# Attention exponentials kept in PSUM, normalised at once and turned by DMA; GpSimd splits the queries and most weights

## The chip, the cores and the metric

The kernel runs on one core of one Trainium2 chip. The time is device microseconds for one execution; the median of three runs of the kernel before is 1127.67 us (1126.69 to 1128.68). In the text PE is TensorE, DVE is VectorE, ACT is ScalarE, POOL is GpSimd and SP is the queue (SyncE) from which most transfers are issued. Each of these works through its own list of instructions in a fixed order and waits where an operand or a buffer is not ready.

## The reference

Two layers of a transformer trunk for 512 latent tokens (an 8 x 64 grid) and 256 context tokens, width 1024. In each layer the tokens are normalised, modulated and multiplied by one wide matrix; its columns feed two parallel attentions and their gates:

```python
px = hx @ w_in
a_k, a_v, b_k, b_v, a_q, b_q, a_z, b_z, g_a, g_b = _split(px, SPLIT_SIZES)
# A: 8 heads of 64, QK-norm; a latent query sees a window of 8 x 16 grid keys
#    with a learned bias, and all 256 context keys
p = jax.nn.softmax(concatenate([s_win, s_ctx]), axis=-1);  a_att = p @ values
# B: 8 query heads, 2 key/value heads, rotary; a latent query sees all 768 keys
s = einsum(q, k) * HEAD_DIM ** -0.5;  p = softmax(s);  b_att = p @ v
o_a = (a_att * silu(a_z)) @ w_o_a;   o_b = (b_att * silu(b_z)) @ w_o_b
merged = sigmoid(g_a) * o_a + sigmoid(g_b) * o_b
x = x + gate * (merged @ w_out)
```

In layer 0 the context tokens are updated too, so their queries (256) attend to the context keys in both branches. In layer 1 only the latent tokens go on. The result has to hold float32 accuracy, so every operand of a product is split into a high and a low half, and a product is two or three matmuls.

## The kernel before, in words

**Stages.** Each layer runs through the projections of keys, values and queries of branch A, the neighbourhood attention (called NA here; in the profile 149.5 to 305.4 us in layer 0 and 771.5 to 881.7 us in layer 1), the projections of branch B, the grouped attention (called GQ; 382.6 to 549.2 us and 938.2 to 1061.3 us), and the merge with the output projection.

**Fill.** PE does not wait for a softmax: `pipeline` (L997) goes over the eight heads, issues the scores of head h, the values of head h-1, and between them a share of `fill`, a list of pieces of projections that nobody needs yet (the gates z, the sigmoid gates g, the output projection of A). A piece is 24 matmuls of 512 or 256 columns (12 for the output projections) into one bank of PSUM (`psf`, `psx`), then an evacuation by ACT and DVE. Its weights come by DMA from the SP queue (`load_w2`, L410): `raw` (three buffers), a rounding copy `whi` on ACT (L418), and the remainder `wlo` = raw - whi (L420), on DVE and POOL in turn (`mix_lo`, L426).

**Order.** The program is written as above, and a planner that simulates the engines then orders the instructions of each engine. Therefore the order of a changed program can differ everywhere.

**NA, one head** (`na_scores`, L938). Four tiles of 128 queries. For each: two matmuls of 512 columns make 256 window scores and 256 context scores in a bank of the pool `pss` (three banks); DVE adds the bias, negates and takes the extreme in one pass from PSUM to an SBUF tile `p` (L958), which frees the bank; ACT does the exponential in place with the row sum (L961); `softmax_tail` scales by half the reciprocal sum, on DVE (L765) or POOL (L768). `na_values` (L968) turns the tiles: three groups of four 128 x 128 blocks go through PE against the identity (L777, L779) into `pst`, and ACT and DVE split each group into a high and a low half (`transpose_split`, L771). Twelve matmuls follow. In layer 0 `ctx_scores` and `ctx_values` do the same for 256 context queries (one group of four blocks). `head_out` (L789) adds the two halves of the result and multiplies it into the gate.

**GQ, one head** (`gq_scores`, L1122). Four tiles of 128 queries by 768 keys, each in a two-bank buffer of `pss` (two buffers). DVE reads it once for the maximum (L1131, it writes a copy that the next line overwrites), ACT writes the exponentials to SBUF (L1132). `turned` (L799) copies them to half precision on ACT (L802), takes the remainder on DVE or POOL in turn (L803), and a DMA transpose from the SP queue (L804) turns both halves. The sums are applied late: `divide` (L806) takes the reciprocals through PE, four blocks for each head and two for the context queries (L811), and multiplies them into the gate on DVE (L812). `shrink` (L815) scales the values of B so that they fit half precision.

**Staging.** `stage_k` and `stage_q` (L840, L849) split the keys and queries of a head: two copies of K (one DVE, one ACT), a remainder on POOL; a copy of Q on ACT and a remainder on DVE (L855).

**PSUM** has eight banks: one `psf`, two `pst` (both for the whole kernel), and five that are dealt out anew for each stage.

## Time and profile before

| | us |
|---|---|
| median of the runs | 1127.67 |
| the profiled execution | 1127.56 |
| its span, first to last instruction | 1125.6 |
| busy: PE / DVE / ACT / POOL | 1093.3 / 774.7 / 579.0 / 490.6 |
| NA, layer 0: length, PE busy | 155.9, 155.9 |
| GQ, layer 0 | 166.6, 151.8 |
| NA, layer 1 | 110.2, 108.7 |
| GQ, layer 1 | 123.1, 118.0 |

A line of the profile names the source line, the engine, the operation, output and inputs with their shapes, the count, then the busy time and the mean of one in ns, and behind the second bar how long the engine had waited just before, and for whom. Matmuls are pipelined: a row of 400 ns is the time through the array, and the next matmul starts before it ends; what one costs is the distance from start to start. A table by windows gives, for each stretch, its length, the busy time of PE, of its weight loads, of DVE, ACT and POOL with the number of instructions, the granted clock, and the share of the DMA engines.

### The profile page before, as it was taken

To read this page: it belongs to the slowest core of one execution; us is meant where nothing else is said; L and a number is where in the kernel's file an instruction comes from. 1 tells how busy PE (TensorE), PEld (TensorE's weight loads), DVE (VectorE), ACT (ScalarE), POOL (GpSimd) and SP (SyncE) were. 2 spreads that over 40 slices of the span, in tenths; PEclk is the share of its full clock that TensorE was granted. 3 is DMA by queue.
4 is the path that set the end of the run, shared out by engine and by line. 5 is a ranking of instruction groups with operands and counts; after the bars stand their busy time and mean duration, and the time that the engine had idled before them with its cause. 6 is when DMAs were issued, how large, how long until landed. Compare 5 with 4: busy or idle time off the path is not lost.

```text
span 1125.6 us, 16862 instructions
## 1 busy us (share of the span) xinstructions
PE 1093.3 (97%) x5826; PEld 905.3 (80%) x5826; DVE 774.7 (69%) x1492; ACT 579.0 (51%) x1154; POOL 490.6 (44%) x405
## 2 busy tenths in 40 slices
PE   8999999999999999979999999999999999999998
PEld 5688888888998877757788888888888987776677
DVE  4666788897466477776577785458878765677473
ACT  6453266665433576755330284326666446776431
POOL 1054254654247144454521545235554563563531
PEclk9999999999999999989999999999999999999999
DMA  9454322242351488869633532553333236989742
GB/s 373 143 172 140 114 63 66 73 136 89 93 168 38 123 201 185 185 172 269 173 108 125 183 129 72 142 174 92 100 107 116 59 105 172 188 224 239 197 145 80
DMA packets 192222, 161.29 MB, mean 143 GB/s; under 512 B 116364, under 2 KB 158088, under 8 KB 190472
## 3 DMA queue, kind: packets, MB, share of 16 engines
q1 hardware_dynamic: 184800, 145.82, 46.8%
q0 software_dynamic: 2368, 7.87, 2.1%
q10 hardware_dynamic: 4968, 6.53, 1.7%
q8 instruction: 46, 0.75, 0.3%
q14 instruction: 40, 0.33, 0.1%
HBM read 115.58 MB, written 17.32 MB: 118 GB/s over the span
## 4 chain that ended last, share of the span: by engine, by line
PE 38%; issue 4%; DVE 3%; DMA 3%; POOL 2%; ACT 1%; SPq 1%; POOLq 0%; ACTq 0%
PE psx L435 6%; PE psx L433 6%; PE psx L434 6%; PE psf L433 4%; PE psf L434 4%; PE psf L435 4%; PE pss L955 1%; PE pss L861 1%; POOL wlo L406 1%; PE pss L862 1%; PE pst L779 1%; PE pst L1148 1%; DMA raw<-in_w_o_a_dram 1%; PE pst L1149 1%; DMA raw<-in_w_in_dram 1%
## 5 line engine op out<-in xcount | busy, mean ns | idle before, releaser
L420 POOL TENSOR_TENSOR wlo<-raw,whi 128x512 fp32r<-128x512 f32 x70 | 97.9, 1405 | 106.1 <-ACT whi L418 70.4
L433 PE MATMUL psf<-hx,whi 128*128 128x512 f32 (+1 forms) x360 | 138.0, 383 | 3.2 <-ACT zt L614 2.4
L435 PE MATMUL psf<-hx,wlo 128*128 128x512 f32 (+1 forms) x360 | 135.8, 377 | 0.0
L434 PE MATMUL psf<-hx,whi 128*128 128x512 f32 (+1 forms) x360 | 135.1, 375 | 0.0
L433 PE MATMUL psx<-whi,hx 128*128 128x512 f32 (+1 forms) x328 | 120.8, 372 | 0.0
L434 PE MATMUL psx<-wlo,hx 128*128 128x512 f32 (+1 forms) x328 | 119.6, 366 | 0.0
L435 PE MATMUL psx<-whi,hx 128*128 128x512 f32 (+1 forms) x328 | 119.5, 365 | 0.0
L418 ACT CAST whi<-raw 128x512 fp32r<-128x512 f32 x136 | 82.3, 620 | 64.0 <-DMA raw<-in_w_in_dram 35.3
L406 POOL TENSOR_TENSOR wlo<-raw,whi 128x512 fp32r<-128x512 f32 x40 | 61.2, 1535 | 122.1 <-ACT whi L403 80.1
L803 POOL TENSOR_TENSOR h<-p,h 128x768 f16<-128x768 f32 (+1 forms) x40 | 65.7, 1644 | 96.4 <-ACT h L802 72.0
L403 ACT CAST whi<-raw 128x512 fp32r<-128x512 f32 x88 | 54.1, 623 | 99.2 <-PE psx L435 34.2
L420 DVE TENSOR_TENSOR wlo<-raw,whi 128x512 fp32r<-128x512 f32 x66 | 73.6, 1115 | 30.6 <-ACT whi L418 29.0
L504 POOL TENSOR_TENSOR ss<-ss,ehalf 128x8 f32<-128x8 f32 (+2 forms) x40 | 62.5, 1566 | 72.9 <-DVE ss L501 72.8
L433 PEld LDWEIGHTS psf<-hx,whi 128*128 128x128 f32 x360 | 67.9, 188 | 15.4 <-ACT zt L614 3.7
L435 PEld LDWEIGHTS psf<-hx,wlo 128*128 128x128 f32 x360 | 67.8, 188 | 11.6
L1131 DVE CUSTOM_DVE_ANT_0 p<-pss,vb 128x768 f32<-128x768 f32 x64 | 60.3, 953 | 23.6 <-PE pss L862 21.1
L434 PEld LDWEIGHTS psf<-hx,whi 128*128 128x128 f32 x360 | 67.9, 189 | 10.3
L1132 ACT ACTIVATE p<-pss,mx 128x768 f32<-128x768 f32 x64 | 57.6, 900 | 34.7 <-DVE mx L1131 33.7
L435 PEld LDWEIGHTS psx<-whi,hx 128*128 128x128 f32 x328 | 61.9, 189 | 10.0
L434 PEld LDWEIGHTS psx<-wlo,hx 128*128 128x128 f32 x328 | 62.0, 189 | 9.2
L433 PEld LDWEIGHTS psx<-whi,hx 128*128 128x128 f32 x328 | 61.8, 189 | 8.9
L435 PE MATMUL psx<-hx,wlo 128*128 128x256 f32 (+1 forms) x208 | 68.0, 327 | 0.0
(362 smaller groups left out, 3095.8 us busy)
## 6 DMA issues: line engine op xcount, KB each, us to landing
raw<-in_w_in_dram SPq DMA_DIRECT2D x168, 256.0 KB, 2.9
rawb<-in_w_ada_dram SPq DMA_DIRECT2D x48, 256.0 KB, 2.8
raw<-in_w_out_dram SPq DMA_DIRECT2D x32, 256.0 KB, 2.9
tg<-gs SPq DMA_DIRECT2D x4, 1536.0 KB, 6.8
rawx<-in_w_ada_dram SPq DMA_DIRECT2D x4, 1024.0 KB, 9.8
rawy<-in_w_ada_dram SPq DMA_DIRECT2D x4, 1024.0 KB, 9.5
gs<-zt ACTq DMA_DIRECT2D x16, 256.0 KB, 2.0
raw<-in_w_o_a_dram SPq DMA_DIRECT2D x16, 256.0 KB, 3.4
```

Source lines behind the costliest of these rows:

```text
L403: S.copy(hi[:, :n], raw[:, :n])
L406: e.tensor_tensor(lo[:, :n], raw[:, :n], F(hi[:, :n]), ALU.subtract)
L418: S.copy(hi, raw)
L420: lo_eng(i).tensor_tensor(lo, raw, F(hi), ALU.subtract)
L433: T.matmul(ps, lhs[0], rhs[0], start=first, stop=False)
L434: T.matmul(ps, lhs[0], rhs[1], start=False, stop=False)
L435: T.matmul(ps, lhs[1], rhs[0], start=False, stop=last)
L504: G.tensor_tensor(ss, ss, ehalf[:, :n], ALU.pow)
L779: T.transpose(pt[:, c0:c0 + 128], src, ident)
L803: eng.tensor_tensor(h[:, 1], p[:, :n], h[:, 0], ALU.subtract)
L1131: V.tensor_tensor_reduce(p, pss, lift, -1.0, 3e38, ALU.add, ALU.min, mx[:, 0:1])
L1132: S.activation(p, pss, AF.Exp, bias=mx[:, 0:1], accum_out=r[:, i:i + 1])
```

## The change

- **NA.** The biased scores and the exponentials stay in the `pss` bank. DVE takes the reciprocal of the sum and multiplies it by 2^14; ACT writes the normalised high half in half precision to SBUF, DVE the remainder, both from PSUM; a DMA transpose from SP turns them (five for each head: the edge tile in two pieces of 64 rows; one more for the context queries in layer 0). The PE transposes and `softmax_tail` are gone. The values of A are kept in half precision, scaled like those of B (`size`, `shrink`, `halves`). Sixteen value matmuls instead of twelve, on the same columns.
- **GQ.** Two tiles of queries share a buffer of three banks (two buffers); one DVE reduction takes both maxima; the exponentials stay there, and are normalised and split as in NA, all remainders on DVE. `divide` is gone. `pst` has one bank in this stage.
- **Values.** `head_out` applies the common scale of the values. The context values of a head are issued after the fill instead of before.
- **Engines.** The remainder of Q goes to POOL; the second copy of K goes from DVE to ACT; for the gates and the output projection of A every `wlo` is made on POOL.

```diff
-    def evac_va(dsts):            # ACT copy, DVE remainder, both float32
+    def size(v, junk, mx):
+        S.activation(junk, v, AF.Abs)
+        V.tensor_reduce(mx, junk, AX, ALU.max)
+    def shrink(mx, s, row):
+        pt = psw(512, "t")
+        T.transpose(pt[0:1, 0:128], mx, ident)
+        V.tensor_reduce(row, pt[0:1, 0:128], AX, ALU.max)
+        T.matmul(pt[:, 128:129], row.to_broadcast([1, 128]), ident[0:1, 0:1], start=True, stop=True)
+        V.tensor_scalar(s[:, 1:2], pt[:, 128:129], 1.0e-30, 1.0 / V_UP, ALU.max, ALU.mult)
+        V.reciprocal(s[:, 0:1], s[:, 1:2])
+        V.tensor_scalar(s[:, 1:2], s[:, 1:2], 0.5 / P_UP, None, ALU.mult)
+    def halves(v, d, s):
+        S.activation(d[:, :, 0, :], v, AF.Copy, scale=s)
+        V.scalar_tensor_tensor(d[:, :, 1, :], v, s, d[:, :, 0, :], ALU.mult, ALU.subtract)
...
-            return fill_chunks(col0, None, gs[c], False, mix_lo)
+            return fill_chunks(col0, None, gs[c], False, pool_lo)
-                    st["w"] = load_w2(src, 256 * i, 4, pool_lo if br == "b" and i == 0 else mix_lo)
+                    st["w"] = load_w2(src, 256 * i, 4, pool_lo if br == "a" or i == 0 else mix_lo)
-        fill = fill_chunks(C_AZ, lambda: za, None, True, mix_lo) + fill_chunks(C_BZ, None, zs, True, mix_lo)
+        fill = fill_chunks(C_AZ, lambda: za, None, True, pool_lo) + fill_chunks(C_BZ, None, zs, True, pool_lo)
...
+    def evac_va(t, ps):
+        S.copy(vf[:, t, :], ps)
+        size(ps, vab[:, 512 * t:512 * t + 512], vmx[:, t:t + 1])
+    def split_va():               # after the first query projection
+        V.tensor_reduce(vmx[:, 6:7], vmx[:, 0:6], AX, ALU.max)
+        shrink(vmx[:, 6:7], vsa, vsa[0:1, 2:3])
+        for t in range(0, 6, 2):
+            halves(vf[:, t:t + 2, :].rearrange("p t (h d) -> p (t h) d", d=64),
+                   va[:, t:t + 2].rearrange("p t h q d -> p (t h) q d"), vsa[:, 0:1])
...
-                S.copy(a, po[o:o + 64, :n])
-                V.tensor_tensor(a, po[m:m + 64, :n], a, ALU.add)
+                S.activation(a, po[o:o + 64, :n], AF.Copy, scale=back[o:o + 64])
+                V.scalar_tensor_tensor(a, po[m:m + 64, :n], back[m:m + 64], a, ALU.mult, ALU.add)
-            def turned(p, n, out, eng):
+            def turned(p, r, cuts, out):
                 h = att["p"].tile([128, 2, n], F16, tag="h", name=nm("h"), bufs=att["nh"])
-                S.copy(h[:, 0], p[:, :n])
-                eng.tensor_tensor(h[:, 1], p[:, :n], h[:, 0], ALU.subtract)
-                nc.sync.dma_start_transpose(out, h.rearrange("p a n -> p (a n)"))
+                for i, (c0, c1) in enumerate(cuts):
+                    V.reciprocal(r[:, i:i + 1], r[:, i:i + 1])
+                    V.tensor_scalar(r[:, i:i + 1], r[:, i:i + 1], P_UP, None, ALU.mult)
+                    S.activation(h[:, 0, c0:c1], p[:, c0:c1], AF.Copy, scale=r[:, i:i + 1])
+                    V.scalar_tensor_tensor(h[:, 1, c0:c1], p[:, c0:c1], r[:, i:i + 1], h[:, 0, c0:c1],
+                                           ALU.mult, ALU.subtract)
+                for o, n0, n1 in out:
+                    nc.sync.dma_start_transpose(o, h[n0:n1].rearrange("p a n -> p (a n)"))
-            def divide(ps, r, e, dst, back):
-            def softmax_tail(p, n, r, pieces, eng=None):
-            def transpose_split(blocks, n0=0, n1=512):
...
-                V.tensor_copy(rows(kh, e), k)
+                S.copy(rows(kh, e), k)
-                V.tensor_tensor(rows(qs, 1 - e), q, F(rows(qs, e)), ALU.subtract)
+                eng.tensor_tensor(rows(qs, 1 - e), q, F(rows(qs, e)), ALU.subtract)   # eng = G
...
             def na_scores(h, q, kh, kl):
-                    p = p_tile()
-                    V.tensor_tensor_reduce(p[:, :512], pss, bedg if i == 0 else bint, -1.0, 3e38,
-                                           ALU.add, ALU.min, mx[:, 0:1])
-                    S.activation(p[:, :512], p[:, :512], AF.Exp, bias=mx[:, 0:1], scale=-1.0, accum_out=r[:, 0:1])
-                    softmax_tail(p, 512, r[:, 0:1], [(0, 512)], G if i in NA_POOL else None)
+                    V.tensor_tensor_reduce(p, p, bedg if i == 0 else bint, -1.0, 3e38,
+                                           ALU.add, ALU.min, mx[:, 0:1])        # p is the PSUM bank
+                    S.activation(p, p, AF.Exp, bias=mx[:, 0:1], scale=-1.0, accum_out=r[:, 0:1])
+                    at = [(0, 64, 0), (448, 512, 64)] if i == 0 else [(128 * i - 64, 128 * i + 64, 0)]
+                    turned(p, r, [(0, 512)], [(ht[:, :, a:b], n, n + b - a) for a, b, n in at])
...
-            open_ps(s=(2, 1024), v=(1, 512))
+            open_ps(t=1, s=(2, 1536))
             def gq_scores(q, kh, kl):
-                for i in range(4):
-                    V.tensor_tensor_reduce(p, pss, lift, -1.0, 3e38, ALU.add, ALU.min, mx[:, 0:1])
-                    S.activation(p, pss, AF.Exp, bias=mx[:, 0:1], accum_out=r[:, i:i + 1])
-                    turned(p, 768, ht[:, i], G if i in SPLIT_POOL else V)
+                for j in range(2):                       # two query tiles in one buffer
+                    V.tensor_reduce(mx, ps.rearrange("p (i n) -> p i n", i=2), AX, ALU.max, negate=True)
+                    for i in range(2):
+                        S.activation(p, p, AF.Exp, bias=mx[:, i:i + 1], accum_out=r[:, i:i + 1])
+                    for i in range(2):
+                        turned(ps[:, 768 * i:768 * i + 768], r[:, i:i + 1], [(0, 768)], [(ht[:, 2 * j + i], 0, 128)])
...
                     st = scores_of(h)
-                    if prev is not None:
-                        values_of(h - 1, prev)
+                    rest = values_of(h - 1, prev) if prev is not None else None
                     run(fill, len(fill) - (n - n * min(h + 1, spread) // spread))
+                    if rest is not None:
+                        rest()                           # the context values
```

More of the change, by code (lines that the diff above doesn't have):

```diff
@@ L759, in layer, with head_out @@
         if True:
[L760 to L789 removed]
+            def head_out(po, e, dst, back, eng=None):
                 n = dst.shape[-1]
@@ L909, in p_tile, with ctx_values @@
-            def p_tile():
-                return att["p"].tile([128, att["w"]], F32, tag="p", name=nm("p"), bufs=att["np"])
+                turned(p, r, [(0, 256), (256, 512)], [(ct.rearrange("p a i k n -> p (a i k) n"), 0, 128)])
+                return ct
+            def ctx_values(ct, vsl, dst, e, back, kind):
+                po = psw(256, kind)
+                for k in range(2):
+                    for a in range(2):
+                        T.matmul(po.rearrange("p (i n) -> p i n", i=2), vsl(4 + k), ct[:, a, :, k, :],
+                                 start=k + a == 0, stop=k + a == 2)
+                head_out(po, e, dst, back)
@@ L993, in na_values @@
+                for t, part in enumerate((((0, 192, 0),), ((64, 192, 1), (192, 320, 0)),
+                                          ((192, 320, 1), (320, 448, 0)), ((320, 512, 1),))):
+                    for n0, n1, k in part:
+                        for a in range(2):
+                            T.matmul(po[:, n0:n1], vsl(t), ht[:, 4 * a + k, n0:n1], start=False,
+                                     stop=t == 3 and a == 1)
                 zv = za.rearrange("p (f n) -> p f n", f=4)
-                head_out(po, e, zv[64 * e:64 * e + 64, h // 2, 0:512], V if h == 7 else G)
+                head_out(po, e, zv[64 * e:64 * e + 64, h // 2, 0:512], vsa[:, 1:2], V if h == 7 else G)
```

238 lines of the change are left out of this document (74 added, 164 removed).

## The prediction

> **What bounds the kernel now.** I read the busy shares first, then a table by windows over the four attentions, then PE's waits.
>
> ```profile
> PE 1093.3 (97%) x5826; PEld 905.3 (80%) x5826; DVE 774.7 (69%) x1492; ACT 579.0 (51%) x1154; POOL 490.6 (44%) x405
> ```
> ```profile
> 149.50:305.40 155.90, 155.90 (x977) 139.22 (x976) 123.15 (x272) 94.01 (x212) 75.67 (x74) 1.00 0.28 87
> 382.60:549.20 166.60, 151.77 (x845) 121.08 (x843) 114.91 (x205) 104.80 (x203) 75.17 (x54) 0.97 0.80 188
> 771.50:881.70 110.20, 108.72 (x595) 93.04 (x594) 93.92 (x186) 72.46 (x151) 57.31 (x57) 1.00 0.33 102
> 938.20:1061.30 123.10, 117.96 (x555) 88.42 (x554) 80.98 (x128) 83.59 (x149) 65.87 (x44) 1.00 0.91 208
> ```
> ```profile
> PE psv L811 <- DVE ho L796: 5.8, 1, 5.8
> PE psf L433 <- ACT zt L614: 4.0, 5, 1.6
> ```
>
> PE is busy throughout both NA stages, and idle for 14.8 us in GQ of layer 0 and 5.1 us in GQ of layer 1. So a matmul removed shortens the kernel by its own distance from start to start, as long as DVE and ACT keep up. In NA, DVE is the second (79% and 85%). The largest single wait, 5.8 us, has this cause:
>
> ```profile
> 492.20 8.26 DVE L420 TENSOR_TENSOR wlo<-raw,whi 128x512 fp32r<-128x512 f32 x1
> ...
> 501.67 0.42 DVE L796 TENSOR_TENSOR ho<-psv,ho 64x256 f32<-64x256 f32 x1
> ```
> ```profile
> 491.54 7.15 POOL L657 TENSOR_TENSOR gal<-za,gah 128x768 fp32r<-128x768 f32 x4
> ```
> ```profile
> 495.00:510.00 15.00, 9.20 (x34) 6.44 (x33) 11.46 (x11) 3.66 (x7) 8.41 (x7) 0.72 0.67 174
> ```
>
> One DVE subtraction with two SBUF operands stood for 8.26 us while POOL worked through four of its own; behind it stood the `head_out` that frees the bank PE wanted. The granted clock then fell to 0.72.
>
> **PE work removed.** The instructions on the identity, by stage, and the distances from start to start:
>
> ```profile
> 149.50:305.40 155.90, 25.40 (x160) 19.34 (x160) 0.00 (x0) 1.00 0.28 87
> 382.60:549.20 166.60, 8.32 (x49) 5.69 (x49) 0.00 (x0) 0.97 0.80 188
> 771.50:881.70 110.20, 18.19 (x128) 14.91 (x128) 0.00 (x0) 1.00 0.33 102
> 938.20:1061.30 123.10, 4.79 (x32) 3.70 (x32) 0.00 (x0) 1.00 0.91 208
> ```
> ```profile
> 247.97 0.28 PE L991 MATMUL psv<-pth,va 128*128 128x256 f32 x1
> 248.09 0.26 PE L992 MATMUL psv<-pth,va 128*128 128x192 f32 x1
> 248.18 0.60 PE L779 MATMUL pst<-ident,p 128*128 128x128 f32 x4
> 248.54 0.48 PE L955 MATMUL pss<-kh,qs 128*128 128x512 f32 x1
> ...
> 250.68 0.39 PE L434 MATMUL psf<-hx,whi 128*128 128x512 f32 x1
> 250.91 0.40 PE L435 MATMUL psf<-hx,wlo 128*128 128x512 f32 x1
> ```
>
> Four transposes take 0.36 us, 0.09 each; 512 columns take 0.23, 256 take 0.12, 192 take 0.09. Transposes: 160 in NA of layer 0 (14.4 us), 128 in layer 1 (11.5), and 48 (one of the 49 belongs to the gates) and 32 from `divide` (4.3 and 2.9). Added: a head's value matmuls were four of 512, four of 192 and four of 256 columns (1.76 us); now four of 512, four of 192 and eight of 128. A 128-column half-precision matmul is in no row; its bounds are 0.06 (a quarter of 512 columns) and 0.09 (192 columns, or a transpose of 128). I take 0.09, the nearest row: 2.0 us, +0.24 a head, +1.9 us a stage. Net on PE: -12.5, -9.6, -4.3, -2.9.
>
> **What a softmax tile now costs DVE and ACT.** The nearest rows, from the groups of NA in layer 1 by shape:
>
> ```profile
> L958 DVE CUSTOM_DVE_ANT_0 p<-pss,bint 128x512 f32<-128x512 f32 x24 | 15.9, 684 | 0.1
> ...
> L762 DVE RECIPROCAL r<-r 128x1 f32<-128x1 f32 x32 | 4.6, 156 | 2.1 <-ACT p L961 1.7
> L796 DVE TENSOR_TENSOR ho<-psv,ho 64x512 f32<-64x512 f32 x6 | 4.1, 682 | 0.6 <-ACT ho L795 0.4
> ...
> L958 DVE DVE_READ_ACCUMULATOR2_ANT mx<- 128x1 f32 x32 | 2.6, 81 | 0.0
> ```
> ```profile
> L961 ACT ACTIVATE p<-p,mx 128x512 f32<-128x512 f32 x32 | 23.0, 720 | 13.7 <-DVE mx L958 13.6
> L418 ACT CAST whi<-raw 128x512 fp32r<-128x512 f32 x20 | 12.1, 616 | 3.3 <-PE psf L434 3.3
> L785 ACT CAST pth<-pst 128x512 fp32r<-128x512 f32 x14 | 7.6, 587 | 0.1
> ...
> L844 ACT CAST kh<-ka 64x768 fp32r<-64x768 f32 x6 | 5.0, 835 | 3.9 <-PE pss L955 3.9
> ```
>
> An NA tile costs DVE 0.68 + 0.08 + 0.16 for the reciprocal, the same for the multiplication by 2^14, and 0.68 for the remainder (from PSUM, as `head_out`): 1.76 us, and 1.93 with a quarter of `head_out`. It costs ACT 0.72 + 0.59 and a quarter of a head's two K copies (0.84 each), Q copy (512 columns, like `whi`, 0.62) and `head_out` copy (like `pth`, 0.59): 2.03 us. Results in PSUM instead of SBUF are in no row: an engine may write there faster or slower, and I take the same durations, because the rows that read from PSUM (684 and 587 ns) stand within 5% of those that read from SBUF with the same columns (616; 682 has one operand in each). The chain of one tile, from scores to remainder, is the sum of its steps, 3.1 us. DVE loses its `wlo`, its Q remainder, one K copy and the scaling on SBUF, and with them the operations that POOL can hold up. POOL gains the Q remainders and 28 `wlo` a layer and loses the scaling and the remainders of GQ; at 49% and 52% in NA it has room for them, and the fill is loaded two pieces ahead.
>
> **NA, layer 0: -11.5.** A head now takes PE some 18 us. ACT had 94.0 us in the stage, 11.8 a head, and gains a K copy and a fourth tile copy: 13.2; DVE, at 15.4 a head, loses more than it gains. So PE stays the bound. In the order of the changed program, fill stands between scores and values up to the last head: after the last tile of head 7 come 8 us of other PE work. The chain from that tile is 0.46 us of matmuls, 3.1 us of steps and 4.2 us of DMA (below), which leaves nothing for the hand-overs between engines. I count 1 us for them: -12.5 + 1.
>
> **NA, layer 1: +6.** Here the new order matters. Between the first scores and the last values 241 fill matmuls are left of 288; 47 now stand before the first scores, where they cost the same. Heads 0 to 3 take most of the rest (67 us of PE work). After the values of head 3 come 13 tiles and the values of four heads with only one piece of 24 x 256 columns among them (2.9 us): 16.7 us of PE work. The tiles go at 2.0 us each on DVE and ACT, 26 us, and then a transpose (4 us) and the last values (2 us): 32 us. So PE idles about 15 us where it had 1.5; with 1 to 2 us for ACT in the first part, -9.6 + 16 = +6. ACT has 62 us there by the rows above (19 exponentials, 18 tile copies, 27 `whi`, 12 evacuations at 0.62, the K and Q copies of five heads, four `head_out`) against 67 of PE. The bounds are -9.6 (ACT and DVE catch up earlier) and +18 (ACT holds up the first part as well).
>
> **GQ.** A pair of tiles now costs one reduction over 1536 columns, two exponentials, two copies and two remainders:
>
> ```profile
> L1131 DVE CUSTOM_DVE_ANT_0 p<-pss,vb 128x768 f32<-128x768 f32 x64 | 60.3, 953 | 23.6 <-PE pss L862 21.1 <-POOL h L803 1.8
> ...
> L874 DVE TENSOR_REDUCE mx<-pss 128x2 f32<-128x512 f32 x16 | 11.0, 686 | 3.4 <-PE pss L862 3.3
> ```
> ```profile
> L804 SPq DMA_TRANSPOSE ht<-h x64: 1274/1678/7132, 388.6 to 1051.1; - x64
> ```
> ```profile
> ht<-h SPq DMA_TRANSPOSE x64, 4.2
> ```
>
> The reduction is between 0.95 (768 columns) and 2.06 us (three times 512); from 512 to 768 each column costs 1.04 ns, which gives 1.75. DVE then has 1.75 + 2 x (0.95 + 0.32) = 4.3 us a pair against 2 x 1.03 and one remainder of 0.95 before, 2.5 more a head; a head's `wlo`, Q remainder and `divide`, which it loses, are some 0.7 to 1 us each: even. ACT's work is the same. The steps of a pair (reduction, two exponentials of 1.5 x 0.72, reciprocals, two copies of 1.5 x 0.59, one remainder) make 7 us, so a buffer is held 8; the order puts 7 to 13 us of PE work between two uses of one, and it is free in time. In layer 0: -4.3, less the 5.8 us wait (its DVE subtraction is gone) and 2.6 us of low clock (0.28 of 9.2), plus 2.7 for `head_out` (1.3 us and its place in two queues), which now stands between two uses of the single `pst` bank, eight times, with 2.8 to 5.5 us of fill: -10 (bounds -15 and +3). In layer 1 the last pair has 8.8 us of PE work behind it, and its chain, 7 us and 4.2 to land, takes some 12 with the hand-overs: -2.9 + 3 = 0 (bounds -4 and +5).
>
> **Elsewhere: +1.** `size`, `split_va` and ACT's `Abs` stand in projections where PE is the bound; PE's two small steps in `shrink` have 4 us of matmuls between them. 0 to +3.
>
> **Sum.** -11.5 + 6 - 10 + 0 + 1 = -14.5. The profiled execution took 1127.56 us, 0.1 below the median of 1127.67: 1113.
>
> **Rivals.**
> 1. *Everything hidden.* If ACT and DVE run ahead of PE in NA of layer 1, its 15 us of idle do not appear: 1098. For it: PE idled 1.5 us there before, and a bunched order need not be a late one if the engines are quicker than I take them. Against: 13 tiles at 2.0 us have only 16.7 us of PE work beside them.
> 2. *The PSUM chain sets the pace* (slower). Before, a score bank was free after one DVE pass of 0.68 us; now it is held through five steps on two engines in turn, 3.1 us and their hand-overs. It decides if the waits in ACT's in-order list stretch a tile from 2.0 to 2.5 us in layer 1 and a head from 13 past 18 us in layer 0. Then layer 0 gains nothing (+12 on the sum) and layer 1 loses 18 (12 more): 1113 + 24 = 1137. For it: in NA of layer 1 ACT has 92% of PE's time in the first part.
> 3. *The SP queue.* 88 more transposes at 1.68 us are 148 us on the queue that also issues every weight load, and each waits there for its remainder; in NA of layer 1 five take 8.4 of a head's 13 us. If the weights of each of 16 heads come 1.2 us late for PE, that is 19 us: 1132. Against: in GQ four a head have stood among loads for 15 us a head.
>    The Trainium skill (VectorE: DVE Perf Modes, "Rules for kernel authors") says to turn 128 x 128 on TensorE when the result may go to PSUM, and by DMA otherwise; its table of the three paths gives 390 ns and 1309 ns. By its figures the two halves of 288 blocks would cost 754 us of DMA against 112 on PE; the trace has twelve blocks landing in 4.2 us, so only the direction of the rule is left, in this rival.
> 4. *No gain on PE.* If a 128-column half-precision matmul cost 0.20 us, a head's values would take 2.9 us and eat most of the transposes: 0.9 x 16 = 14 us on the sum, 1127. Against: a transpose with 128 columns takes 0.09.
>
> **How the numbers follow.** Chances: forecast 0.48, rival 1 0.22, rival 2 0.17, rival 3 0.08, rival 4 0.05. Faster is the forecast and rival 1: 0.70; same (within 0.2%, 2.3 us, about what a measurement of this kernel can tell from no change) rival 4: 0.05; slower 0.25. The forecast's own range is 1103 to 1122; the range over the cases reaches from just under rival 1 to just under rival 2: 1096 to 1136.
>
> **What would show it.** In the windows: NA of layer 0 near 144 us with PE full; in layer 1 a stretch of some 30 us before the first projection of B with PE half idle and waiting for DMA `ht` or for DVE and ACT on `pss`; no DVE instruction of several us in GQ; no wait above 2 us on `pst`. Wrong would be: PE waits on `raw` or `wlo` in NA (rival 3), DVE or ACT rows on PSUM well above those used here (rival 2), or layer 1 without the idle stretch (rival 1).

## The result, and the profile after

The changed kernel takes 1139.07 us (median of four runs, 1137.48 to 1141.67) against 1127.69 for the kernel before beside it: a ratio of 1.0103, 95% interval 1.0082 to 1.0124. It is slower by 1%, where 1113 was forecast. The profiled execution is the slowest of the four (1141.67); its span is 1139.6 us, 14.0 more than before, where the medians differ by 11.4.

Line 1 of the page of the changed kernel, and its table by windows from the first scores to the last values of NA and GQ in layer 0, then in layer 1 (length; busy time of PE, its weight loads, DVE, ACT, POOL; granted clock; DMA share; GB/s):

```profile
PE 1067.9 (94%) x5528; PEld 857.5 (75%) x5528; DVE 698.8 (61%) x1498; ACT 626.1 (55%) x1208; POOL 485.2 (43%) x389
```
```profile
154.60:305.60 151.00, 140.92 (x863) 118.35 (x862) 100.23 (x280) 104.54 (x226) 68.85 (x57) 0.99 0.76 167
...
378.80:542.90 164.10, 148.68 (x809) 115.26 (x807) 111.66 (x234) 110.97 (x212) 58.13 (x45) 0.98 0.86 194
...
778.50:886.90 108.40, 90.93 (x452) 68.92 (x451) 65.14 (x176) 78.03 (x152) 49.08 (x36) 0.91 0.80 176
...
948.40:1075.20 126.80, 112.11 (x504) 80.22 (x503) 81.24 (x131) 86.80 (x147) 51.68 (x41) 0.99 0.87 201
```

PE's work did fall, by 25.4 us (1093.3 to 1067.9). Its idle time rose by 39.4 (span less busy: 32.3 to 71.7). The lengths of the stages mislead, because the planner moved fill from one stage to the next; length less PE busy does not. Against the forecast's terms (the profiled executions; the forecast's -5.7 for GQ of layer 0 holds 2.6 us of low clock, which the measured columns have under busy):

| term of the sum | forecast, us | measured, us | off by |
|---|---|---|---|
| PE busy, all stages | -29.3 | -25.4 | 3.9 |
| PE idle, NA of layer 0 | +1 | +10.1 | 9.1 |
| PE idle, GQ of layer 0 | -5.7 | +0.6 | 6.3 |
| PE idle, NA of layer 1 | +15.6 | +16.0 | 0.4 |
| PE idle, GQ of layer 1 | +2.9 | +9.6 | 6.7 |
| PE idle, elsewhere | +1 | +3.1 | 2.1 |
| sum | -14.5 | +14.0 | 28.5 |

PE's waits in the changed kernel, longest in total first (total, times, longest):

```profile
PE pst L931 <- DMA ht<-h: 12.1, 3, 6.7
PE psf L429 <- ACT zt L617: 10.1, 10, 2.4
PE pss L912 <- DVE h L798: 5.6, 5, 3.1
PE psf L429 <- DVE tg L695: 4.4, 5, 2.0
PE pst L1094 <- DVE ho L787: 4.0, 1, 4.0
```

**NA, layer 0.** Three times PE stands at `psf` for more than 1 us (2.25, 1.10 and 1.28 of the 5.3 us there), and each time ACT's list shows the same picture. From the timeline of the changed kernel:

```profile
194.55 0.66 ACT L917 ACTIVATE pss<-pss,mx 128x512 f32<-128x512 f32 x1 [4.63 <-DVE mx L914]
...
195.23 0.82 ACT L818 CAST kh<-ka 64x768 fp32r<-64x768 f32 x1
...
196.08 0.83 ACT L819 CAST kh<-ka 64x768 fp32r<-64x768 f32 x1
...
196.93 0.84 ACT L829 CAST qs<-qa 64x768 fp32r<-64x768 f32 x1
...
199.60 0.58 ACT L617 ACTIVATE zt<-psf 128x512 f32<-128x512 f32 x1
...
200.35 0.69 DVE L619 SCALAR_TENSOR_TENSOR zt<-zt,psf 128x512 f32<-128x512 f32 x1
```
```profile
201.09 0.50 PE L429 MATMUL psf<-hx,whi 128*128 128x512 f32 x1 [2.25 <-DVE zt L619]
```

The next head's two K copies and its Q copy run 2.5 us in a row on ACT, and the evacuation that gives PE its bank back comes after them (in this case after an exponential, a `head_out` copy and a context exponential as well). Just before, ACT had been idle for 4.63 us: its load was not the limit. Before the change, the first K copy was on DVE.

**NA, layer 1.** The tail, in windows and in its last tile:

```profile
844.30:886.90 42.60, 25.13 (x122) 15.82 (x122) 25.80 (x71) 26.39 (x52) 11.21 (x8) 0.76 0.74 140
850.00:880.00 30.00, 17.36 (x72) 9.86 (x72) 21.54 (x64) 21.04 (x43) 9.18 (x7) 0.77 0.78 142
```
```profile
866.53 15.34 SPq L801 DMA_TRANSPOSE ht<-h  x8
...
877.10 0.70 DVE L914 CUSTOM_DVE_ANT_0 pss<-pss,bint 128x512 f32<-128x512 f32 x1 [2.21 <-PE pss L912]
...
879.86 0.75 DVE L798 SCALAR_TENSOR_TENSOR h<-pss,r,h 128x512 f16<-128x512 f32 x1 [0.81 <-ACT h L797]
...
883.78 1.86 PE L931 MATMUL pst<-ht,va 128*128 128x512 f16 x4 [6.72 <-DMA ht<-h]
```

As forecast in kind: 30 us in which PE is busy for 17.4 and DVE and ACT for 21 each, and the last values behind the transposes. The first row is the whole stretch behind the values of head 3, 42.6 us long.

**GQ, layer 0.** The 8.26 us DVE instruction is gone, and a wait of the same form stands elsewhere: now ACT's list is behind a late weight, and the `head_out` that frees `pst` behind that. The weight was issued at 478.75 and landed 12.4 us later, where the median of its line is 3.1; ahead of it on SP stood two loads of the gates (`tg`, 1.5 MB each, landed by 488.9), not transposes.

```profile
477.32 1.33 SPq L663 DMA_DIRECT2D tg<-gs  x2
478.75 0.38 SPq L411 DMA_DIRECT2D raw<-in_w_o_a_dram  x1
...
491.16 0.62 ACT L414 CAST whi<-raw 128x512 fp32r<-128x512 f32 x1 [3.15 <-DMA raw<-in_w_o_a_dram]
491.69 0.87 ACT L1079 ACTIVATE pss<-pss,mx 128x768 f32<-128x768 f32 x1
...
492.70 0.47 ACT L786 ACTIVATE ho<-pst,vb 64x256 f32<-64x256 f32 x1
...
493.75 0.51 PE L1094 MATMUL pst<-ht,vb 128*128 128x512 f16 x1 [3.96 <-DVE ho L787]
```

**GQ, layer 1.** One pair of tiles at the end of the stage, from its reduction to its second remainder:

```profile
1057.34 1.75 DVE L1075 TENSOR_REDUCE mx<-pss 128x2 f32<-128x1536 f32 x1
...
1064.39 0.90 ACT L797 ACTIVATE h<-pss,r 128x768 f16<-128x768 f32 x1
...
1065.32 1.02 DVE L798 SCALAR_TENSOR_TENSOR h<-pss,r,h 128x768 f16<-128x768 f32 x1
1066.38 0.90 ACT L797 ACTIVATE h<-pss,r 128x768 f16<-128x768 f32 x1 [1.09 <-DVE h L798]
...
1067.31 1.02 DVE L798 SCALAR_TENSOR_TENSOR h<-pss,r,h 128x768 f16<-128x768 f32 x1 [0.97 <-ACT h L797]
...
1068.47 0.47 PE L429 MATMUL psx<-gbh,whi 128*128 128x512 f32 x1 [2.58 <-DVE h L798]
```

The pair takes 11.0 us (1057.34 to 1068.33), where the forecast had 7 to the first remainder and 8 to the second. It is no exception: over the 16 pairs of this stage the median is 10.5 us (8.5 to 14.1), over those of layer 0 10.1. Two things are new. ACT waits with the copies while its list stands at a `head_out`, and the second tile's copy waits until the first tile's remainder has ended, although it reads other columns: the two tiles share the middle bank. The Trainium skill (PSUM — Partial Sum Buffer, "PSUM bank collisions raise a hardware error") says that two engines may not touch one bank in the same quadrant of 32 partitions at once, reads included, and that the compiler back end's scheduler adds a dependency between two such instructions. The wait of 1.09 us agrees with it.

### The profile page after: what moved, and what is told of

Its sections match the earlier page's. It is cut to its first block, busy times and chain, and to the rows that moved or that the text cites. A ratio compares the mean times of both kernels' runs of the same rounds, so it can differ in the third digit from the quotient of the medians.

```text
span 1139.6 us, 16576 instructions
## 1 busy us (share of the span) xinstructions
PE 1067.9 (94%) x5528; PEld 857.5 (75%) x5528; DVE 698.8 (61%) x1498; ACT 626.1 (55%) x1208; POOL 485.2 (43%) x389
## 5 line engine op out<-in xcount | busy, mean ns | idle before, releaser
L416 POOL TENSOR_TENSOR wlo<-raw,whi 128x512 fp32r<-128x512 f32 x126 | 166.1, 1333 | 131.4 <-ACT whi L414 77.5
L798 DVE SCALAR_TENSOR_TENSOR h<-pss,r,h 128x768 f16<-128x768 f32 (+2 forms) x160 | 127.0, 801 | 36.8 <-ACT h L797 34.8
L429 PE MATMUL psf<-hx,whi 128*128 128x512 f32 (+1 forms) x360 | 137.6, 382 | 12.4 <-ACT zt L617 9.6
L797 ACT ACTIVATE h<-pss,r 128x768 f16<-128x768 f32 (+2 forms) x160 | 114.2, 729 | 26.1 <-DVE h L798 15.7
L402 POOL TENSOR_TENSOR wlo<-raw,whi 128x512 fp32r<-128x512 f32 x40 | 59.5, 1489 | 130.2 <-ACT whi L399 86.0
L1075 DVE TENSOR_REDUCE mx<-pss 128x2 f32<-128x1536 f32 x32 | 55.9, 1754 | 42.4 <-PE pss L837 42.3
L431 PEld LDWEIGHTS psf<-hx,wlo 128*128 128x128 f32 x360 | 68.2, 189 | 12.4
L429 PE MATMUL psx<-hx,whi 128*128 128x256 f32 (+1 forms) x208 | 68.3, 328 | 0.0
```

The lines of the kernel that those rows point to most:

```text
L402: e.tensor_tensor(lo[:, :n], raw[:, :n], F(hi[:, :n]), ALU.subtract)
L416: lo_eng(i).tensor_tensor(lo, raw, F(hi), ALU.subtract)
L429: T.matmul(ps, lhs[0], rhs[0], start=first, stop=False)
L431: T.matmul(ps, lhs[1], rhs[0], start=False, stop=last)
L797: S.activation(h[:, 0, c0:c1], p[:, c0:c1], AF.Copy, scale=r[:, i:i + 1])
L798: V.scalar_tensor_tensor(h[:, 1, c0:c1], p[:, c0:c1], r[:, i:i + 1], h[:, 0, c0:c1], ALU.mult, ALU.subtract)
```

## The experiments

Each ran against the kernel before on the same chip, in three rounds (the last one in five); times are medians. Three chips served in all; the kernel before took 1126.9 to 1127.3 us on each. Idle times are of one execution, the profiled one, which can lie some us from the median. The planner orders every kernel anew, so a single stage also carries chance: with the same code and the moves, the GQ of before idles 11.1 us in layer 0 beside the old NA and 17.1 beside the new one (161.50 less 150.38, 168.30 less 151.19).

### The three parts, alone and together

```diff
-    return fill_chunks(col0, None, gs[c], False, mix_lo)       # and the z fills, o_chunks "a"
+    return fill_chunks(col0, None, gs[c], False, pool_lo)
-    V.tensor_copy(rows(kh, e), k)
+    S.copy(rows(kh, e), k)
-    V.tensor_tensor(rows(qs, 1 - e), q, F(rows(qs, e)), ALU.subtract)
+    G.tensor_tensor(rows(qs, 1 - e), q, F(rows(qs, e)), ALU.subtract)
```


> The kernel before with the engine moves alone (wlo of the gates and of the output projection of A on POOL, the remainder of Q on POOL, the second copy of K on ACT); both attentions as before. Theory A (the loss sits in the attentions: after the change PE is idle 17.5 us in NA of layer 1 and 14.7 us in GQ of layer 1, against 1.5 and 5.1): the moves alone change little, 1122 to 1130 us. Rival B (the moves are the loss: a wlo takes 1.3 us on POOL against 0.7 on DVE and the weights come late): 1134 us or more here, and the two other parts alone come out below 1125.

Measured: 1126.62 us, 1.0004 (0.9991 to 1.0017). The moves alone cost nothing, as theory A said.

```diff
 # the kernel before, with the changed na_scores, na_values, ctx_scores, evac_va, split_va
-    pipeline(fill, 9, na_first, values_of(za, na_values), bg=bg)
+    pipeline(fill, 9, na_first, values_of_a(za, na_values, vsa[:, 1:2], "v"), bg=bg)
```


> The kernel before with the neighbourhood attention alone changed (scores and exponentials in PSUM, DMA transposes, half-precision values), engines and GQ as before. Theory A: the stage of layer 0 gains 2 to 3 us, that of layer 1 loses about 6 to its bunched tail, and some 2 us go elsewhere: 1130 to 1136 us, with PE idle 10 us or more in NA of layer 1. Rival B (engine moves are the loss): below 1120 us.

Measured: 1122.99 us, 0.9954 (0.9939 to 0.9969): faster, and outside what either theory expected. NA of layer 0 and of layer 1 in that run:

```profile
149.70:295.10 145.40, 142.28 (x886) 121.37 (x885) 117.49 (x307) 101.13 (x223) 49.60 (x42) 1.00 0.80 176
...
767.80:880.00 112.20, 93.96 (x489) 73.69 (x488) 84.69 (x196) 73.36 (x146) 33.55 (x22) 0.94 0.77 170
```

145.4 us with 3.1 idle is what the forecast had for layer 0 (near 144), and 18.2 us idle in layer 1 is its bunched tail.

```diff
 # the kernel before, with the changed gq_scores, gq_values, ctx_scores, split_vb
-    open_ps(s=(2, 1024), v=(1, 512))
+    open_ps(t=1, s=(2, 1536))
```


> The kernel before with the grouped attention alone changed (pairs of tiles in three banks, exponentials in PSUM, no divide, one pst bank), engines and NA as before. Theory A: layer 0 gains some 4 us, layer 1 loses some 7: 1128 to 1134 us. Rival B (engine moves are the loss): 1115 to 1122 us.

Measured: 1143.76 us, 1.0137 (1.0107 to 1.0166). More than either theory: GQ, without the moves, is the largest single loss. Its two stages are idle for 21.3 and 18.5 us, with DVE at 129 us in layer 0 (115 before):

```profile
382.30:559.30 177.00, 155.72 (x846) 122.48 (x845) 129.07 (x251) 111.21 (x213) 40.81 (x31) 0.97 0.79 180
942.30:1080.70 138.40, 119.86 (x527) 87.09 (x526) 92.06 (x145) 88.32 (x150) 38.16 (x28) 0.96 0.84 189
```

```diff
 # the changed kernel, with gq_scores, gq_values, divide and the banks of before
```


> The changed kernel with the grouped attention of before (single tiles in two banks, exponentials in SBUF, remainders on DVE and POOL, divide); the neighbourhood attention and the engine moves stay changed. Theory D (the loss is in GQ alone, and the other two parts add up): stages near those of the runs with one part, 147, 162, 112 and 120 us, and 1118 to 1124 us in all. Rival E (the parts hinder each other, since POOL's longer list now makes the weights late for the faster NA): 1130 us or more.

Measured: 1141.85 us, 1.0124 (1.0105 to 1.0142). The parts don't add: the moves cost nothing beside the old NA and 19 us beside the new one.

```diff
 # the changed kernel, with na_scores, na_values, evac_va of before
```


> The changed kernel with the neighbourhood attention of before: the GQ change together with the engine moves. Measured so far, against before: engine moves alone 1.000, NA alone 0.995, GQ alone 1.014, NA with the engine moves 1.012, all three 1.010. Theory H (the engine moves heal what the GQ change loses, since they empty DVE there, and hurt only the changed NA): 1122 to 1130 us here, with GQ of layer 1 near 124 us. Rival I (GQ's own chain is the loss, whatever DVE has besides): 1138 to 1144 us, GQ of layer 1 130 us or more.

Measured: 1133.74 us, 1.0063 (1.0045 to 1.0081), between the two theories. With the moves the GQ change loses 7 us (1126.62 to 1133.74), without them 16; its stage in layer 1 stays 15.1 us idle (125.80 less 110.67). So beside the new GQ the moves gain 10 us, where beside the new NA they cost 19. NA with GQ and without the moves was not run.

### What the moves do to NA

```diff
-    S.copy(rows(kh, e), k)
+    (S.copy if dup else V.tensor_copy)(rows(kh, e), k)         # dup: GQ
-    q = stage_q(qav[:, j, :], e, G)
+    q = stage_q(qav[:, j, :], e, V)
-    return fill_chunks(col0, None, gs[c], False, pool_lo)
+    return fill_chunks(col0, None, gs[c], False, mix_lo if c < n_na else pool_lo)   # z fills: mix_lo
```


> The changed kernel with the engine moves undone in the neighbourhood attentions alone: there the wlo of the fill alternates between POOL and DVE, the first copy of K and the remainder of Q are on DVE; in GQ they stay moved. Theory H (the moves hurt the changed NA: ACT's list, with two more copies a head and the evacuations, holds PE): NA of layer 0 falls from 151 to 145 us as in the run with NA alone, and the time to 1120 to 1128. Rival I: no stage changes by more than 3 us, 1135 to 1142.

Measured: 1132.43 us, 1.0048 (1.0028 to 1.0069), NA of layer 0 at 144.7 us. The stage does what theory H said; the time falls by 6.6, less than the 11 or more that it had. NA of layer 1 idles 21.0 us here (17.5 in the changed kernel).

```diff
 # as above, with pool_lo for the gates and the z fills, as in the changed kernel
```


> As the run that undoes all the engine moves in NA, but only the copy of K and the remainder of Q go back to DVE; every wlo stays on POOL. If the K and Q moves are what hurts (ACT 6.6 us more a stage, scores late by the slower Q remainder on POOL): the same time as that run within 3 us. If it is the wlo on POOL (1.3 us each, one behind the other, so fill comes late): the time of the changed kernel, 1136 to 1141.

Measured: 1132.04 us, 1.0046 (1.0018 to 1.0074): the same, though its ten runs reach from 1122.8 to 1137.5. So it is K and Q; within this the `wlo` on POOL are free in NA, as forecast. PE no longer waits on `psf` in NA of layer 0; of its 5.0 us of idle 4.7 are a wait for `ht`.

```diff
-    q = stage_q(qav[:, j, :], e, G)
+    q = stage_q(qav[:, j, :], e, V)
```


> The changed kernel, in NA only the remainder of Q back on DVE; the first copy of K stays on ACT. With both back it took 1132. If the Q remainder on POOL is what cost (1.8 us there in layer 0, in a queue with the wlo, and scores wait for it): 1130 to 1134. If the two copies of K on ACT are (0.83 us each, sixteen heads): 1137 to 1141.

Measured: 1136.76 us, 1.0073 (1.0049 to 1.0098), between the two expectations. By the medians Q on POOL has 2.3 us of the 7.0 and the K copies on ACT 4.7, but the interval of this run overlaps those of both others. In NA of layer 0, Q back on DVE is enough: 5.2 us idle, with the K copies still on ACT.

```profile
152.00:299.60 147.60, 142.43 (x877) 121.09 (x876) 108.46 (x289) 104.90 (x228) 59.77 (x51) 0.99 0.78 171
```

### The order in NA of layer 1

```diff
     st = scores_of(h)
+    behind(ON_PE, lambda: run(fill, m))       # layer 1: a head's fill pinned behind its scores
     rest = values_of(h - 1, prev) if prev is not None else None
-    run(fill, m)
```


> The changed kernel, with one thing else: in NA of layer 1 each head's share of fill is pinned on PE behind that head's scores (and the values stand after it), so that no fill can move ahead of its head; operations and buffers are the same. Theory A (the 17.5 us of idle come from the order alone: too little PE work left beside the last four heads): idle in the stage falls below 5 us and the time to 1122 to 1128 us. Rival C (the chain in PSUM sets the pace, ACT's list is too full): the idle spreads over the heads, and the time stays at 1135 to 1140 us.

Measured: 1165.90 us, 1.0331 (1.0309 to 1.0352), worse than either theory. The planner put three tiles' scores in a row, then the fill, and PE stood at the fourth; the stage idles 29.9 us:

```profile
PE pss L912 <- DVE h L798: 25.8, 9, 4.8
```

There are three banks, and from the bias pass to the remainder a tile took 5.1 us in the median there (3.9 to 8.2; in the changed kernel 5.8, and 3.5 at the least; each of DVE's 32 passes paired with its remainder), not 3.1. The 7 us in the next expectation are not that median.

```diff
 # layer 1; each piece of fill in two halves of 12 matmuls (k 0 to 3 and 4 to 7)
     for i in range(4):
         p = ps_score()
-        scores(p, qi, kh, kl, ...)
+        behind(ON_PE, lambda: na_tile(p, qi, kh, kl, i))
+        behind(ON_PE, lambda: run(fill, m))           # m: what the tile's 32nd part comes to
```


> The changed kernel, with NA of layer 1 ordered tile by tile: half a piece of fill (2.8 us of PE) is pinned on PE behind the scores of each tile, and the next tile's scores behind it. Theory A (the idle of this stage comes from fill that has moved away from the last four heads): PE idle in the stage falls from 17.4 us below 5, and the time to 1124 to 1130. Rival C (even with one tile at a time the chain through ACT's and DVE's lists, 7 us in the run that pinned whole heads, holds the three banks for too long): waits of PE on pss stay above 10 us, and the time is 1135 or more.

Measured: 1133.71 us, 1.0054 (1.0036 to 1.0072), 5.4 less than the changed kernel, between the two expectations. The stage's idle falls from 17.5 to 5.3 us, that of the whole kernel only from 71.7 to 66.4:

```profile
762.30:876.70 114.40, 109.13 (x546) 86.83 (x547) 66.03 (x179) 84.31 (x162) 58.48 (x43) 0.96 0.82 176
```

Part of it came back ahead of the stage, where the fill had covered the first Q remainder: PE waits 6.6 us for it there, and 750 to 762.3 us is busy for 3.1.

### What holds GQ

```diff
-    for j in range(2):
-        ps = ps_score(1536)                  # two tiles, two buffers of three banks
+    for i in range(4):
+        p = ps_score(768)                    # one tile, three buffers of two banks
```


> The changed kernel, in GQ with one tile of 768 columns to a buffer: three buffers of two banks in place of two of three, one reduction, exponential, copy and remainder for each; one pst bank as in the changed kernel. Theory F (the pair is the cause: a buffer is held through the steps of two tiles, and only two heads' halves are in flight): GQ of layer 1 falls from 126.8 to 118 to 121 us, of layer 0 from 164 to 155 to 160, and the time to 1122 to 1130. Rival G (the DVE work is the cause, all remainders and reductions on one engine with in-order waits): less than 4 us in all, 1135 to 1141.

Measured: 1134.43 us, 1.0069 (1.0054 to 1.0084): 4.6 less than the changed kernel, where theory F had at least 9. The lengths of the stages came close to it (121.7 and 159.6 us), but the idle time fell by 4.0 us in layer 1 and rose by 0.7 in layer 0. ACT's waits with a copy for a remainder, in the changed kernel (GQ of layer 1, then layer 0) and in this one (layer 0; there is none above 0.3 us in layer 1):

```profile
ACT h L797 <- DVE h L798: 4.9, 6, 1.1
...
ACT h L797 <- DVE h L798: 10.0, 13, 1.8
```
```profile
ACT h L797 <- DVE h L798: 2.2, 5, 0.6
```

Of the 14.9 us in the changed kernel, 10.7 belong to the tiles of 768 columns, which now have none; the other 4.2 are context tiles, two of which still share a bank, like the 2.2 here. So the wait at a shared bank is real. What it costs by itself is not shown: with one tile to a buffer, a buffer is also held for less (6.3 us in the median in layer 1, against 10.5).

```diff
-    S.activation(p, p, AF.Exp, ...)                          # p: ps[:, 768 * i:...]
+    p = att["p"].tile([128, 768], F32, tag="p", ...)         # SBUF; NH_GQ (3, 4)
+    S.activation(p, ps[:, 768 * i:768 * i + 768], AF.Exp, ...)
```


> The changed kernel, in GQ with the exponentials written to SBUF, as before the change, so that a pair's three banks are free after the second exponential instead of after the second remainder; everything else (pairs, early normalising, remainders on DVE, one pst bank) as in the changed kernel; fewer buffers for h (3 and 4) make room. Theory F (the time for which PSUM is held is the cause): GQ of layer 1 falls to 118 to 122 us and the time to 1125 to 1132. Rival G (DVE's list is the cause): 1136 to 1145, no gain, or a loss from DVE sharing SBUF with POOL.

Measured: 1143.32 us, 1.0142 (1.0124 to 1.0160). The time is theory G's, and its loss is in the remainder: from SBUF it takes 1220 ns in the mean of layer 0, from PSUM 1015. The median is 1017, though: the 34 of the 64 that overlap no instruction of POOL take 1.01 us, the other 30 1.54. GQ of layer 1 does what theory F said (9.6 us idle, 14.7 in the changed kernel), that of layer 0 does not (19.2 against 15.4). Freeing the banks early did not pay here.

```profile
L798 DVE SCALAR_TENSOR_TENSOR h<-p,r,h 128x768 f16<-128x768 f32 x32 | 38.9, 1220 | 7.6 <-ACT h L797 7.4
...
L798 DVE SCALAR_TENSOR_TENSOR h<-p,r,h x64: 994/1017/2633, 385.6 to 1046.6; 128x768 f16<-128x768 f32 x64
```

```diff
 # single tiles as above
-    open_ps(t=1, s=(3, 1024))
+    open_ps(x=1, t=2, s=(2, 1024))            # two score buffers, two banks for fill, two for values
```


> The changed kernel with single tiles in GQ, and the banks there dealt out otherwise: two buffers of two banks for scores (three in the run before), two banks for fill (one before) and two for values (one before). If the one bank for fill is what PE waits on in GQ (7.6 us on psf for ACT and 3.3 for DVE in layer 0): idle in GQ falls below 10 us in layer 0, and the time from 1134 to 1122 to 1129. If the score buffers are: waits on pss grow, and the time is 1134 to 1145.

Measured: 1199.70 us, 1.0646 (1.0618 to 1.0674). In GQ of layer 0 PE's waits on `psf` for ACT's `zt` (7.6 us in the run before) are gone, so the single bank was behind them; but with two buffers instead of three the chain in PSUM sets the pace, and GQ idles 31.0 and 40.6 us. The waits of the whole kernel:

```profile
PE pss L836 <- DVE h L798: 24.9, 11, 5.3
PE pst L1091 <- DMA ht<-h: 19.4, 7, 7.8
```

### Repairs together, and kernels that beat both

```diff
 # the changed kernel + K and Q on DVE in NA + single tiles in GQ + tile-wise order in NA of layer 1
```


> The changed kernel with three repairs at once, each run singly before: the copy of K and the remainder of Q back on DVE in NA (7 us less alone), single tiles in GQ (5 less alone), NA of layer 1 pinned tile by tile (5 less alone). If the causes are separate they add: 1139 - 17 = 1122 us, 1118 to 1126. If each repair only shifts the same wait on to the next stage: 1130 or more.

Measured: 1121.60 us, 0.9946 (0.9931 to 0.9961). The three repairs, 7.0, 4.6 and 5.4 us alone, give 17.5 together. In GQ of layer 1 the idle falls to 6.3 us (in layer 0 it is 18.0):

```profile
933.60:1055.00 121.40, 115.07 (x523) 85.73 (x522) 82.54 (x147) 86.46 (x150) 53.76 (x42) 0.99 0.91 211
```

```diff
 # the kernel with NA changed alone + tile-wise order in NA of layer 1
```


> The kernel before with NA changed alone (1123 us), and in layer 1 the fill pinned tile by tile as in the run that did so with the changed kernel (there 5 us less). If the idle in NA of layer 1 (18.2 us) is due to the order: 1110 to 1118 us, the stage's idle below 10. If DVE, with its wlo and the Q remainder, cannot keep the pace that the pinned order asks: 1123 to 1130.

Measured: 1119.15 us, 0.9935 (0.9915 to 0.9955), between the two expectations; the interval overlaps that of NA alone. The stage's idle falls from 18.2 to 6.3 us, but that of the whole kernel only from 51.1 to 49.2: most of it turns up elsewhere, 4.7 us as a wait for the first Q remainder ahead of this stage's first scores.

```diff
 # that kernel, and in GQ alone: wlo of the last gates and of w_o_a on POOL, K copy on ACT, Q remainder on POOL
```


> NA changed and pinned (1119 us), GQ as before, and the engine moves in GQ alone (wlo of the last gates and of the output projection of A, remainder of Q, copy of K). If the moves relieve DVE in GQ as they did alone (GQ of layer 0 from 166.8 to 161.5): 1112 to 1117. If what a stage idles is set by the evacuations of fill and not by DVE: 1117 to 1124.

Measured: 1114.21 us, 0.9886 (0.9870 to 0.9903), with the next one the fastest. The time is what was expected if the moves help, but not the place: GQ of layer 0 idles as before, that of layer 1 for 3.1 us (5.1 in the pinned kernel).

```profile
369.10:535.90 166.80, 150.95 (x845) 120.89 (x843) 112.63 (x191) 104.79 (x203) 97.89 (x68) 0.96 0.73 188
...
927.40:1040.30 112.90, 109.76 (x525) 83.01 (x524) 66.44 (x113) 82.30 (x147) 80.43 (x55) 1.00 0.87 215
```

```diff
 # the pinned kernel; in GQ:
-    open_ps(s=(2, 1024), v=(1, 512))
+    open_ps(x=1, s=(2, 1024))                 # a second bank for fill; values share pst
```


> NA changed and pinned (1119 us), the GQ of before on DVE and POOL as before, and there two banks for fill and none for psv (the values share the two banks of pst). If the one bank for fill keeps GQ idle: the 15.9 us of layer 0 fall below 10, 1110 to 1116 us. If not, or if the shared value banks cost as much: 1118 to 1126.

Measured: 1114.56 us, 0.9892 (0.9865 to 0.9919). GQ of layer 0 idles 10.7 us (16.3 in the pinned kernel): here a second bank for fill helps. A likely reason, not run by itself: the exponentials of that GQ leave PSUM at once, so that two score buffers are enough.

```diff
 # the pinned kernel, with the edits of both kernels above
```


> NA changed and pinned, GQ of before, with both the engine moves in GQ (1114.2 alone) and two banks for fill there (1114.6 alone, from 1119). If they help in different places: 1107 to 1112. If both only remove the same wait: 1112 to 1118.

Measured: 1119.29 us, 0.9941 (0.9920 to 0.9962). They don't add; why was not followed up.

## Why the prediction was wrong

- **The direction.** The forecast and the rival "everything hidden" held 0.70, and both were wrong. The time was nearest to rival 2 (1137), but its mechanism, the chain in PSUM pacing NA, is not what happened: PE waited 5.6 us for a score bank there, and NA alone is faster than before. Nearness to its number is luck, although its condition for layer 1, 2.5 us a tile, did hold in the tail (below). The chain sets the pace where buffers are taken away (whole heads in a row, or two buffers in GQ).
- **PE work removed: right in kind.** -25.4 against -29.3. The part of NA alone came to -26.6 with a forecast of -22.1, that of GQ alone to -2.5 with -7.2. The low granted clock in idle stretches (0.76 in the tail above) gives some back. The 128-column matmul is cheap, so rival 4 falls: twelve value matmuls take 0.94 us from first start to last end, against 1.08 in the sum.

```profile
803.09 0.94 PE L936 MATMUL pst<-ht,va 128*128 128x192 f16 x12
```

- **Tile costs: slightly low.** DVE came to 2.08 us a tile (forecast 1.93) and ACT to 2.28 (2.03). The remainder and the copy from PSUM to half precision are slower than the rows taken for them (682 and 587), and ACT's read-out of the sum was left out, though it stood in the trace of the kernel before (189 ns). The chain of a tile was forecast as the sum of its steps, 3.1 us, and took 5.8 in the median: the steps alone come to 3.5, the least of the 32, and waits between them add the rest. For NA of layer 1:

```profile
L798 DVE SCALAR_TENSOR_TENSOR h<-pss,r,h 128x512 f16<-128x512 f32 x32 | 23.5, 748 | 6.6 <-ACT h L797 6.4
L797 ACT ACTIVATE h<-pss,r 128x512 f16<-128x512 f32 x32 | 21.4, 687 | 0.5 <-ACT pss L917 0.5
...
L917 ACT ACTIVATION_READ_ACCUMULATOR pss<-pss,mx 128x1 f32 x32 | 6.3, 196 | 0.0
```

- **NA, layer 0: the step that failed is "ACT gains a K copy ... 13.2; so PE stays the bound".** The load was right (104.5 us in the stage, 13.1 a head). But a copy was costed as load and not as a place in ACT's list, ahead of the evacuation that frees the only `psf`. With K and Q back on DVE the stage's idle falls from 10.1 to 5.0 us and the waits on `psf` from 5.3 to none; without any of the moves it is 3.1. With Q alone back it is 5.2, in a new order: so the row of three copies in ACT's list does not explain it alone, and how it and the slower Q remainder work together is not settled. "POOL has room" was right for `wlo` and too simple for Q. The hand-over at the end was also counted short: 1 us against 3.2 and 0.5 for `ht`.
- **NA, layer 1: right in mechanism and place, the size in part by luck.** Behind the values of head 3 stood just what was forecast: 13 tiles, the values of four heads and one piece of fill. But the stretch took 42.6 us and not 32: from the first bias pass in it (846.95) to the last (877.10) a tile took 2.5 us, not 2.0, with neither DVE nor ACT full. PE was busy for 25.1 us of it and not 16.7, at a granted clock of 0.76 (25.1 x 0.76 is an estimated 19 us at full clock). The two errors all but cancel in the idle time, +16.0 against +15.6. The two runs that took moves back left the idle there (21.0 and 16.0 us); the tile-wise order removed 12 us of it and gave some back before the stage.
- **GQ, layer 0: the term "-5.8 and -2.6" failed.** The DVE instruction that caused the wait did go, and the single `pst` was priced at 2.7, but what would be late next was not named: ACT's list, at a weight that came late behind the gates' loads (3.96 us of PE), and `psf` behind ACT and DVE (4.7 and 3.3 us in the stage). "No wait above 2 us on `pst`" was wrong.
- **GQ, layer 1: the step "the steps of a pair make 7 us, so a buffer is held 8" failed.** 10.5 us in the median, 11.0 for the pair shown: the shared bank puts copy, remainder, copy, remainder one behind the other, and ACT's list interposes a `head_out`. "DVE even" held, as load: 111.7 us against 114.9 in layer 0, 81.2 against 81.0 in layer 1. It holds only with the moves: without them DVE has 129 us in layer 0, and the GQ change loses 16 us where with them it loses 7. How the 7 divide between the shared bank, the longer hold and the order of ACT's list is open.
- **SP (rival 3): as forecast.** No PE wait on weights appeared in NA. In the tail eight transposes stand in a row on the queue, 15.34 us from the first issue to the end of the last. The weight that came late in GQ of layer 0 stood behind the gates' loads, not behind transposes.
- **The rule on transposes.** The Trainium skill (VectorE: DVE Perf Modes, "Rules for kernel authors") would have kept them on TensorE, since their result may go to PSUM. The run with NA alone shows the other side: with PE as the bound, the change of NA, which takes 288 of them off it, made the kernel 0.46% faster, tails included.

Open are the split between K and Q, and why NA with the moves is as slow with the GQ of before (1141.85) as with the changed one: of the 23 us between the two profiled executions (19 between the medians), 14.3 are idle PE and 8.7 busy time at a clock of 0.979 instead of 0.989. Of the idle, 8.1 us are in NA of layer 0, as in the changed kernel; NA of layer 1 has 4.8 less, GQ has 1.0 more in layer 0 and 4.0 in layer 1, and 6.0 lie outside the four stages. The largest single wait is 8.2 us on a score bank in GQ. Open, too, is what takes the rest of the GQ change's loss.

## What to carry to other kernels

Price a moved instruction twice, as load and as a place in its new engine's list: ask which evacuation stands behind it, and how many banks the bound engine has to bridge it; a stall that goes names its successor in the same way. When results stay in PSUM through several steps, count the buffers against the time that each is held: here they became the bound before any engine's load did, and two tiles that shared a bank took turns. Run the parts of a compound change alone before judging the whole: here NA made the kernel faster and GQ slower, and the moves cost nothing alone, 19 us beside the new NA, and gained 10 beside the new GQ.

## What the runs showed that was not expected

- ACT's copy waited for DVE's remainder of other columns in the same bank of PSUM: 14.9 us of ACT idle in the two GQ stages, 2.2 with one tile to a bank pair.
- One score buffer fewer in GQ cost 65 us (1134.43 to 1199.70), although fill and values had a bank more each.
- An exponential with a row sum is followed by a read-out of 0.20 us on ACT (0.19 in the kernel before, where the forecast passed over it).
- The remainder of a GQ tile takes 1.01 us from PSUM, and from SBUF 1.01 where POOL is idle and 1.54 in the mean where POOL works.
- The same GQ code, ordered anew beside another NA, differs by 6 us of idle in one stage (11.1 and 17.1).
